# Two latent key/value blocks and two query blocks of a mixer as one Strassen quad ahead of the gate quads, with the convolution blocks regrouped

## The chip, the cores and the metric

The kernel runs on one core of one Trainium2 chip. The metric is the time of one execution in device microseconds. The engines are named as the profile names them: PE is TensorE, DVE is VectorE, ACT is ScalarE, POOL is GpSimd, SP issues the loads.

## The reference, cut to what matters

The trunk has two layers (DEPTH 2) over 512 tokens of width 1024. Each layer is a half-step SwiGLU, a mixer, a second half-step SwiGLU, and a per-layer embedding. The change is in the front of the mixer:

```
u = rmsnorm(h, mix_norm[i])
b_g, c_g, v_c, q_c, kv_c, k_r, g_conv, g_mla = jnp.split(u @ w_in[i], split_pts, axis=-1)
y_conv = short_conv_branch(b_g, c_g, v_c, conv_w[i], w_conv_out[i])
y_mla = mla_branch(q_c, kv_c, k_r, q_norm[i], kv_norm[i], ...)     # rmsnorm of q_c and kv_c first
merged = jax.nn.sigmoid(g_conv) * y_conv + jax.nn.sigmoid(g_mla) * y_mla
```

In blocks of 128 columns, w_in holds four blocks each for B, C and V of the convolution, three for the query latent q_c, two for the key/value latent kv_c, half a block for the rotary key k_r, and eight for each of the two gates. The output is the final RMSNorm of h, 512 x 1024.

## The kernel before, in words

Activations lie transposed: a block is 128 channels by 512 tokens. Each fp32 number is split into a rounded part (hi) and a rest (lo), so a plain projection of one block (`proj`, L275, and `mm3`, L266 to L270) is eight channel groups times three matmuls of 512 columns: hi with hi, hi with lo, lo with hi.

Weights come in tiles of 128 x 1024 (eight 128 x 128 blocks). SP loads them into ten raw buffers `st`; `Stream.split` (L58 to L73) makes `wh` with a cast on ACT (L71) and `wl` with a subtraction on DVE (L72). There are four buffers of `wh` and four of `wl`, so a split waits until PE has finished with the tile four before it.

A **quad** is a block of four output columns computed by a seven-product Strassen scheme over halves of the channels and halves of the tokens. `Quad.part` (L138 to L158) makes its seven weight tiles from four raw ones: seven splits, and four additions or subtractions of 128 x 1024 on DVE (L149, L152, L154, L157). `Sevens.step(n, j)` (L552) does product j of quad n in the order 1, 2, 6, 5, 7, 3, 4. Products 1, 2, 6, 3 and 4 are `joint` (L516): eight matmuls of 512 columns (L525) and eight of 256 (L529). Products 5 and 7 are `product` (L532): 24 matmuls of 256 columns (L538). Two of the sums are started by a **seed**: ACT copies 128 x 1024 from one PSUM buffer `b` into the buffer `a` or `d` (L543), both of which are the single buffer of the pool `ap`. Product 2 adds into `a` and so waits for its seed; product 5 adds into `d` and waits for its own. A seed also waits until DVE has read out what that buffer held before (L548). After product 2, 3 and 4, ACT copies one half (L547), DVE adds the other (L548) and scales by the row norm r; gates then go through a sigmoid on ACT. The token sums and differences that the quads read as moving operand come from `Halved.row` (L457 to L496): four subtractions or additions of 128 x 256 and three splits per row on DVE, and five operations on ACT, for four rows.

The mixer (`mixer`, L736) starts with the two kv blocks (L768), the rotary key (L771 to L776) and the mean square of h (`rms`, L340), whose result r scales all that follows. Then the three query blocks, the norms of the two latents (`lat_norm`, L760: a mean square through two matmuls, an inverse root on ACT, then scaling on DVE), and convolution blocks 0 to 3, each C, V, B. Product 1 of quad 0 stands after C of block 3, products 2 and 6 after its V. Four quads of gates follow, `step(n+1, 1)`, `step(n, 4)`, `step(n+1, 2)` and so on, with the projections of the convolution's output (`conv_out`, L806) between them.

PSUM has eight banks here: `bp` (two buffers of two banks, the `b` of the quads; also lent to convolution blocks), `ap` (one of two banks) and `mp` (two of one bank, `PS`). A tile of `PS` waits for the reader of the tile whose bank it takes. Instructions of one engine run in the order in which Tile's scheduler has put them; each engine's queue is strictly in that order.

Of the kernel before, what the change touches and what calls it, by code (L numbers as in the profile page):

```python
# [13 lines left out]
ALU = mybir.AluOpType  # L14
AX = mybir.AxisListType

P = 128
# [3 lines left out]
ROPE = 64  # L21
# [3 lines left out]
SCALE = float((NOPE + ROPE) ** -0.5)  # L25
# [157 lines left out]
def trunk_kernel(ctx, tc, dims, x, p, positions, gains, rope_c, final_row, weights, out):  # L183

    nc = tc.nc
# [14 lines left out]
    def G(name, dt=F32):  # L200
        return gp.tile([P, S], dt, tag="g", name=name)
# [28 lines left out]
    def PS(name):  # L230
        return banks.single.tile([P, 512], F32, tag="mm", name=name)
# [4 lines left out]
    def PB(name):  # L236
        return two(banks.chain, name)
# [4 lines left out]
    def halves(t):  # L242
        return [t[:, 0, :], t[:, 1, :]]
# [28 lines left out]
    def proj(tiles, vs, name, ps=None):  # L272
        ps = PS(name) if ps is None else ps
        o = ps[:, :vs[0][0].shape[1]]
        for k, (t, v) in enumerate(zip(tiles, vs)):  # L275
            mm3(o, W.get(t), v, k == 0, k == len(tiles) - 1)
        return ps

    def projs(cols_, vs, pss, part_by_part=False):

        for k, (vh, vl) in enumerate(vs):
            ws = [W.get(tiles[k]) for tiles in cols_]
            if k == 0 and part_by_part:
                for ps, (wh, _) in zip(pss, ws):
                    nc.tensor.matmul(ps, wh, vh, start=True, stop=False)
                for ps, (_, wl) in zip(pss, ws):
                    nc.tensor.matmul(ps, wl, vh, start=False, stop=False)
                for ps, (wh, _) in zip(pss, ws):
                    nc.tensor.matmul(ps, wh, vl, start=False, stop=False)
                continue  # L290
            for ps, w in zip(pss, ws):
                mm3(ps, w, (vh, vl), k == 0, k == len(vs) - 1)
        return pss
# [22 lines left out]
    def gain(nm, l, k):  # L316
        c = col_at[nm, l] + k
        return cols[:, c:c + 1]
# [23 lines left out]
    def rms(acc, n, name, scale=1.0, ps=None):  # L342

        ah, al = acc
        ps = PS(name + "ps") if ps is None else ps
        nc.tensor.matmul(ps, ones, ah, start=True, stop=False)
        nc.tensor.matmul(ps, ones, al, start=False, stop=True)
        r, t, ms = (rp.tile([P, S], F32, tag=g, name=name + w) for g, w in (("r", "r"), ("w", "t"), ("w", "ms")))

        nc.scalar.activation(r, ps, AF.Abs_reciprocal_sqrt, scale=1.0 / n, bias=eps_t)  # L350
        nc.scalar.activation(t, r, AF.Square)
        nc.scalar.activation(ms, ps, AF.Identity, scale=1.0 / n, bias=eps_t)
        nc.vector.scalar_tensor_tensor(t, t, -0.5 * scale, ms, ALU.mult, ALU.mult)
        nc.vector.scalar_tensor_tensor(r, t, 1.5 * scale, r, ALU.add, ALU.mult)
        return r
# [369 lines left out]
    def rope(src, cos, sin, name):  # L725

        t1, t2 = G(name + "t1"), G(name + "t2")
        for a in range(0, P, 64):
            for o, i in ((a, a + 32), (a + 32, a)):
                nc.scalar.copy(t2[o:o + 32, :], src[i:i + 32, :])  # L730
        nc.vector.tensor_tensor(t1, src, cos, ALU.mult)
        nc.vector.tensor_tensor(t2, t2, sin, ALU.mult)
        nc.vector.tensor_tensor(t1, t1, t2, ALU.add)
        return t1

    def mixer(l):  # L736
# [7 lines left out]
        o_gc = o_kr + ROPE  # L744
        o_gm = o_gc + D

        def lat_in(c0, width, nm):
            pss = halves(PB(f"{name}{nm}p")) + [PS(f"{name}{nm}p2")]
            return [proj(W.col("w_in", l, c0 + k * P, D), xs, None, pss[k]) for k in range(width // P)]

        def lat_scale(pss, nm):
            ts, sq = [], Squares(name + nm)
            for k, ps in enumerate(pss):
                t = G(f"{name}{nm}t{k}")
                nc.vector.tensor_tensor(t, ps, r, ALU.mult)
                ts.append(t)
                sq.add(t)
            return ts, sq.parts()

        def lat_norm(ts, acc, nm, scale=1.0):  # L760
            rl = rms(acc, len(ts) * P, name + nm, scale)
            for k, t in enumerate(ts):
                nc.vector.scalar_tensor_tensor(t, t, gain(nm, l, k), rl, ALU.mult, ALU.mult)
            return ts

        pkv = halves(PB(name + "kvp"))
        projs([W.col("w_in", l, o_kv + k * P, D) for k in range(KL // P)], xs, pkv)

        pkr = PS(name + "krp")
        kr_cols = W.col("w_in", l, (o_kr, o_kr), D)  # L770
        for k, (vh, vl) in enumerate(xs):  # L771
# [3 lines left out]
            nc.tensor.matmul(pkr, wa[:, t], vh, start=k == 0, stop=False)  # L775
            nc.tensor.matmul(pkr, wb[:, t], vl, start=False, stop=k == KD - 1)  # L776
        r = rms(acc, D, name)
        kvt = lat_scale(pkv, "kv")
        krn, krs = G(name + "krn"), G(name + "krs")
        nc.scalar.copy(krs[:ROPE, :], pkr[ROPE:, :])  # L780
        nc.vector.tensor_tensor(krs[:ROPE, :], pkr[:ROPE, :], krs[:ROPE, :], ALU.add)
        for o in (0, ROPE):
            nc.vector.tensor_tensor(krn[o:o + ROPE, :], krs[:ROPE, :], r[:ROPE, :], ALU.mult)
        qt = lat_scale(lat_in(o_q, QL, "q"), "q")
        kvt = lat_norm(*kvt, "kv")
        krt = rope(krn, cosT, sinT, name + "kr")
        ys = Halved("mix", l, name)


        yc = []  # L790
        r2 = G(name + "r2")
        nc.vector.tensor_tensor(r2, r, r, ALU.mult)

        gates = [None] * (2 * KD)

        def gate(n, f, c, src, t):
            at = slice(c * (S // 2), (c + 1) * (S // 2))
            nc.vector.tensor_tensor(t, src, r[:, at].unsqueeze(1).to_broadcast([P, 2, S // 2]), ALU.mult)
            for w in range(2):
                i = 4 * n + 2 * f + w  # L800
                if gates[i] is None:
                    gates[i] = G(f"{name}g{i}")
                nc.scalar.activation(gates[i][:, at], t[:, w, :], AF.Sigmoid)

        def conv_out(m):
            ps = proj(W.col("w_conv_out", l, m * P, CONV), yc, f"{name}cop{m}")  # L806
            nc.vector.tensor_tensor(gates[m], ps, gates[m], ALU.mult)


        step = Sevens("w_in", l, name + "g", ys.ys,  # L810
                      lambda n: [[o_gc + (4 * n + 2 * a_ + w) * P for w in range(2)] for a_ in range(2)], gate).step

        for k in range(CONV // P):
            last = k == CONV // P - 1
            pc = PS(f"{name}Cp{k}") if last else halves(PB(f"{name}Cp{k}"))[0]
            ps = proj(W.col("w_in", l, o_c + k * P, D), xs, None, pc)
            c = G(f"{name}c{k}")
            nc.vector.tensor_tensor(c, ps, r2, ALU.mult)
            if last:
                ys.row(k, xs)  # L820
                step(0, 1)
            ps = proj(W.col("w_in", l, o_v + k * P, D), xs, f"{name}Vp{k}")
            z = G(f"{name}z{k}")
            nc.vector.tensor_tensor(z, ps, c, ALU.mult)
            y = G(f"{name}y{k}")
            cw = [gain("conv", l * 3 + j, k) for j in range(3)]
            nc.scalar.mul(y, z, cw[2])
            nc.vector.scalar_tensor_tensor(y[:, 1:], z[:, :-1], cw[1], y[:, 1:], ALU.mult, ALU.add)
            nc.vector.scalar_tensor_tensor(y[:, 2:], z[:, :-2], cw[0], y[:, 2:], ALU.mult, ALU.add)
            if last:  # L830
                step(0, 2)
                step(0, 6)
            ps = proj(W.col("w_in", l, o_b + k * P, D), xs, f"{name}Bp{k}")
            b = G(f"{name}b{k}")
            nc.vector.tensor_tensor(b, ps, r, ALU.mult)
            nc.vector.tensor_tensor(y, y, b, ALU.mult)
            yc.append(split(y, f"{name}yc{k}"))
            if not last:
                ys.row(k, xs)
            if k == 1:  # L840
                qt = lat_norm(*qt, "q", SCALE)
        for j in (5, 7, 3):
            step(0, j)

        class Pair:
            def __init__(self, pr):
# [54 lines left out]
                assert self.vw or not nxt  # L901

        pairs = [Pair(pr) for pr in range(N_HEADS // 2)]
        n_last = KD // 2 - 1
        outs = list(range(KD - 1))

        def conv_outs(n):
# [2 lines left out]
            del outs[:n]  # L910

        for n in range(n_last):
            for n_, j_, n_out in ((n + 1, 1, n > 0), (n, 4, 0), (n + 1, 2, 0), (n + 1, 6, 1), (n + 1, 5, 0), (n + 1, 7, 0),
                                  (n + 1, 3, 1)):
                step(n_, j_)
                conv_outs(n_out)
                if (n_, j_) == (n_last, 2):
                    qc = [split(t, f"{name}qn{k}", paired=True) for k, t in enumerate(qt)]
                    kvc = [split(t, f"{name}kvn{k}") for k, t in enumerate(kvt)]
                    krh, krl = split(krt, name + "kr", paired=True)  # L920
# [356 lines left out]
```

## Time and profile before

| | |
|---|---|
| median of 3 runs | 2260.66 us (2260.35 to 2261.06) |
| the profiled execution, its own time | 2260.81 us |
| its span, first to last instruction | 2258.7 us |
| PE busy | 2246.9 us, 99% of the span |
| DVE busy | 1719.7 us, 76% |
| ACT busy | 1432.2 us, 63% |
| weight load of PE (PEld) | 1947.6 us, 86% |
| granted TensorE clock | 0.999 |
| the mixer of layer 0, first matmul of kv to start of product 1 of quad 0 | 351.88 to 438.58 us |
| the mixer of layer 0, from there to the last product of quad 3 | 438.58 to 549.50 us |

The ends of matmuls are modelled, so PE is read by the distance from one start to the next. The idle time of an engine other than PE costs nothing by itself. The lines that matter are shown in the prediction.

### The profile page before, as it was taken

To read this page: it belongs to the slowest core of one execution; us is meant where nothing else is said; L and a number is where in the kernel's file an instruction comes from. 1 tells how busy PE (TensorE), PEld (TensorE's weight loads), DVE (VectorE), ACT (ScalarE), POOL (GpSimd) and SP (SyncE) were. 2 spreads that over 40 slices of the span, in tenths; PEclk is the share of its full clock that TensorE was granted. 3 is DMA by queue.
4 is the path that set the end of the run, shared out by engine and by line. 5 is a ranking of instruction groups with operands and counts; after the bars stand their busy time and mean duration, and the time that the engine had idled before them with its cause. 6 is when DMAs were issued, how large, how long until landed. Compare 5 with 4: busy or idle time off the path is not lost.

```text
span 2258.7 us, 30986 instructions
## 1 busy us (share of the span) xinstructions
PE 2246.9 (99%) x12080; PEld 1947.6 (86%) x12080; DVE 1719.7 (76%) x2423; ACT 1432.2 (63%) x2220; POOL 37.3 (2%) x42
## 2 busy tenths in 40 slices
PE   9999999999999999999999999999999999999998
PEld 7888888888888888888888888888888888888887
DVE  8887767877876877776798777678879678777756
ACT  7666666566744666666676666655567457666664
POOL 0000000000200000000000000000001000000000
PEclk9999999999999999999999999999999999999999
DMA  5233332223122223333222333332322223333321
GB/s 215 96 105 103 112 122 95 73 95 102 48 103 84 88 99 103 104 112 131 84 94 95 102 105 110 112 103 75 103 75 75 94 75 103 102 105 105 111 94 38
DMA packets 63363, 223.05 MB, mean 99 GB/s; under 512 B 7280, under 2 KB 7280, under 8 KB 63216
## 3 DMA queue, kind: packets, MB, share of 16 engines
q1 hardware_dynamic: 62640, 220.28, 29.2%
q8 instruction: 95, 1.56, 0.3%
q10 hardware_dynamic: 576, 0.79, 0.1%
q14 instruction: 52, 0.43, 0.1%
HBM read 218.94 MB, written 2.10 MB: 98 GB/s over the span
## 4 chain that ended last, share of the span: by engine, by line
PE 99%; ACT 0%; DVE 0%; issue 0%; DVEq 0%; ACTq 0%
PE b1pd L268 2%; PE b0pd L268 2%; PE a1pd L268 2%; PE a0pd L268 2%; PE a1pd L269 2%; PE b0pd L269 2%; PE b1pd L269 2%; PE b1pd L270 2%; PE a1pd L270 2%; PE b0pd L270 2%; PE a0pd L269 2%; PE a0pd L270 2%; PE m0mop L268 1%; PE m0mop L269 1%; PE m1mop L268 1%; PE m1mop L270 1%
## 5 line engine op out<-in xcount | busy, mean ns | idle before, releaser
L72 DVE TENSOR_TENSOR wl<-st,wh 128x1024 fp32r<-128x1024 f32 (+1 forms) x504 | 610.2, 1213 | 322.4 <-ACT wh L71 321.4
L71 ACT CAST wh<-st 128x1024 fp32r<-128x1024 f32 (+1 forms) x503 | 523.8, 1044 | 420.5 <-issue 13.8
L152 DVE TENSOR_TENSOR st<-st,st 128x1024 f32<-128x1024 f32 x47 | 57.5, 1224 | 1.3
L72 DVE TENSOR_TENSOR wl<-s,wh 128x1024 fp32r<-128x1024 f32 x47 | 57.2, 1217 | 0.4 <-ACT wh L71 0.4
L154 DVE TENSOR_TENSOR s<-st,st 128x1024 f32<-128x1024 f32 x47 | 57.3, 1219 | 0.2
L149 DVE TENSOR_TENSOR st<-st,s 128x1024 f32<-128x1024 f32 x47 | 57.2, 1216 | 0.0
L157 DVE TENSOR_TENSOR st<-st,st 128x1024 f32<-128x1024 f32 x47 | 57.1, 1216 | 0.0
L71 ACT CAST wh<-s 128x1024 fp32r<-128x1024 f32 x47 | 48.9, 1041 | 8.2 <-PE a1p L269 2.6
L632 ACT ACTIVATE h<-a0pd 128x512 f32<-128x512 f32 x40 | 23.7, 596 | 17.7 <-PE a0pd L270 17.6
L632 ACT ACTIVATE h<-b1pd 128x512 f32<-128x512 f32 x40 | 23.8, 597 | 16.9 <-PE b1pd L270 16.7
L632 ACT ACTIVATE h<-a1pd 128x512 f32<-128x512 f32 x40 | 23.7, 596 | 16.5 <-PE a1pd L270 16.3
L632 ACT ACTIVATE h<-b0pd 128x512 f32<-128x512 f32 x40 | 23.7, 596 | 16.4 <-PE b0pd L270 16.3
L628 ACT ACTIVATE a0pd<-h 128x512 f32<-128x512 f32 x40 | 24.0, 601 | 2.5 <-DVE a010o L548 1.7
L628 ACT ACTIVATE b1pd<-h 128x512 f32<-128x512 f32 x40 | 24.0, 602 | 2.2 <-DVE b110o L548 1.4
L628 ACT ACTIVATE a1pd<-h 128x512 f32<-128x512 f32 x40 | 24.0, 601 | 2.2 <-DVE a110o L548 1.4
L628 ACT ACTIVATE b0pd<-h 128x512 f32<-128x512 f32 x40 | 24.0, 601 | 2.2 <-DVE b010o L548 1.4
L107 POOL MEMSET wh<- 128x256 f32 x4 | 1.1, 312 | 1180.6 <-DVE wl L72 1180.6
L270 PE MATMUL a0p<-a0x,wl 128*128 128x512 f32 x44 | 17.1, 389 | 0.0
L268 PE MATMUL a0p<-a0x,wh 128*128 128x512 f32 x44 | 17.1, 389 | 0.0
L269 PE MATMUL a0p<-a0x,wh 128*128 128x512 f32 x44 | 17.1, 389 | 0.0
L263 ACT ACTIVATE b0x<-h,cols 128x512 fp32r<-128x512 f32 x8 | 5.8, 724 | 13.3 <-DVE h L1027 13.3
L263 ACT ACTIVATE b1x<-h,cols 128x512 fp32r<-128x512 f32 x8 | 5.8, 724 | 13.3 <-DVE h L1027 13.3
(6807 smaller groups left out, 7498.1 us busy)
## 6 DMA issues: line engine op xcount, KB each, us to landing
st<-in_weights SPq DMA_DIRECT2D x406, 512.0 KB, 3.3
h<-in_x SPq DMA_DIRECT2D x8, 256.0 KB, 5.5
st<-in_weights SPq DMA_DIRECT2D x7, 256.0 KB, 5.4
out<-e1d SPq DMA_DIRECT2D x4, 256.0 KB, 2.1
out<-fh SPq DMA_DIRECT2D x3, 256.0 KB, 2.3
e0pi<-in_p SPq DMA_DIRECT2D x2, 256.0 KB, 4.5
e1pi<-in_p SPq DMA_DIRECT2D x2, 256.0 KB, 4.4
fg<-in_final_row SPq DMA_DIRECT2D x2, 256.0 KB, 5.3
```

Source lines behind the costliest of these rows:

```text
L71: self.nc.scalar.copy(hi[:, w], src[:, w])
L72: self.nc.vector.tensor_tensor(lo[:, w], src[:, w], hi[:, w].bitcast(F32), ALU.subtract)
L149: tt(self.a12, self.a12, self.s, ALU.subtract)
L152: tt(self.a11, self.a11, self.a21, ALU.subtract)
L154: tt(self.s, self.a22, self.a11, ALU.subtract)
L157: tt(self.a21, self.a21, self.a22, ALU.add)
L263: nc.scalar.activation(hi, src, AF.Copy, scale=scale)
L268: nc.tensor.matmul(ps, wh, vh, start=first, stop=False, skip_group_check=seeded)
L269: nc.tensor.matmul(ps, wh, vl, start=False, stop=False, skip_group_check=seeded)
L270: nc.tensor.matmul(ps, wl, vh, start=False, stop=last, skip_group_check=seeded)
L628: nc.scalar.mul(ps, h[m], 2.0)
L632: nc.scalar.mul(h[m], ps, 0.5)
```

## The change: what it does

It takes the two kv blocks and the first two query blocks out of the plain projections and makes them quad 0; the four quads of gates become quads 1 to 4 (`n_last` goes from 3 to 4). The third query block stays a plain projection (`pq2`) and now opens the mixer, ahead of the rotary key. The rows of `Halved` are made during convolution blocks 0 and 1. Blocks 0 and 1 stand ahead of quad 0; C, V and B of block 2 stand after products 1, 2 and 6 of quad 0, those of block 3 after products 1, 2 and 6 of quad 1. C of blocks 2 and 3 takes a `PS` bank; before, only block 3's did. The mean squares and norms of the two latents move behind products 6, 5, 7 and 3 of quad 1. Everything is done in both layers.

```diff
-        pkv = halves(PB(name + "kvp"))
-        projs([W.col("w_in", l, o_kv + k * P, D) for k in range(KL // P)], xs, pkv)
+        pq2 = proj(W.col("w_in", l, o_q + 2 * P, D), xs, None, halves(PB(name + "qp"))[0])
...
-        qt = lat_scale(lat_in(o_q, QL, "q"), "q")
-        kvt = lat_norm(*kvt, "kv")
...
+            if n == 0:
+                for w in range(2):
+                    nc.vector.tensor_tensor(lats[2 * f + w][:, at], src[:, w, :], r[:, at], ALU.mult)
+                return
...
+            cs = [o_kv, o_kv + P, o_q, o_q + P] if n == 0 else [c0 + i * P for i in range(4)]
...
+            pc = halves(PB(f"{name}Cp{k}"))[0] if k < 2 else PS(f"{name}Cp{k}")
...
+        for j in (1, 2, 6, 5, 7, 3):
             step(0, j)
+            if j in (1, 2, 6):
+                next(convs[2])
...
-        n_last = KD // 2 - 1
+        n_last = KD // 2
...
-                conv_outs(n_out)
+                if n == 0:
+                    if j_ in (1, 2, 6):
+                        next(convs[3])
+                    if j_ == 6:
+                        kva = latents(kvt, "kv")
+                    if j_ == 5:
+                        qa = latents(qt, "q")
+                    if j_ == 7:
+                        lat_norm(kvt, kva, "kv")
+                    if j_ == 3:
+                        lat_norm(qt, qa, "q", SCALE)
+                else:
+                    conv_outs(n_out)
```

**ACT, up to the seed of the second gate quad.** Before, this is the stretch in which quad 0 (gates) ends and quad 1 begins: `m0g0` is quad 0, `m0g1a` the seed that product 2 of quad 1 waits for, `wh` a weight cast, L803 the sigmoids.

```order
L71 CAST wh_4292<-st_4014 128x1024
L566 COPY m0g0c_4198<-m0g0d 128x512
L71 CAST wh_4318<-st_4267 128x1024
L71 CAST wh_4349<-s 128x1024
L803 ACTIVATE m0g_4230<-m0g0c_4198 128x256
L803 ACTIVATE m0g_4232<-m0g0c_4198 128x256
L547 COPY m0g0o_4255<-m0g0d 128x512
L71 CAST wh_4374<-st_4372 128x1024
L543 COPY m0g1a<-m0g1b 128x1024
```

In the changed kernel the same stretch lies between quad 1 (now the first gates) and quad 2; `m0kv` and `m0q` belong to the norms of the latents, L776 are the sigmoids, and the seed is `m0g2a`.

```order
L350 ACT_TABLE_LOAD
L350 ACTIVATE m0kvr<-m0kvps,eps_t 128x512
L260 CAST m0qah<-m0qacc 128x512
L351 ACTIVATE m0kvt<-m0kvr 128x512
L776 ACT_TABLE_LOAD
L776 ACTIVATE m0g_4271<-m0g1c_4227 128x256
L776 ACTIVATE m0g_4273<-m0g1c_4227 128x256
L352 ACTIVATE m0kvms<-m0kvps,eps_t 128x512
L547 COPY m0g1o_4309<-m0g1d 128x512
L71 CAST wh_4417<-s 128x1024
L547 COPY m0g1o_4380<-m0g1b 128x512
L543 COPY m0g2a<-m0g2b 128x1024
```

Two loads of an activation table and the norm of the kv latent now stand in ACT's queue ahead of the seed, where there were casts, one pair of sigmoids and one copy; a second such pair of loads, for the query latent, stands between this seed and the next one (`m0g2d`).

**DVE, up to the reader of V of convolution block 1.** Before, between the reader of its C (L818) and of its V (L824) stands one weight split.

```order
L470 TENSOR_TENSOR m0t_3668<-m0x_3667 128x256
L484 TENSOR_TENSOR m0t_3668<-m0y_3673,m0x_3667 128x256
L485 TENSOR_TENSOR m0u_3674<-m0t_3668,m0x_3667 128x256
L486 TENSOR_TENSOR m0u_3674<-m0y_3673,m0u_3674 128x256
L261 TENSOR_TENSOR m0t0l<-m0t_3668,m0t0h 128x512
L261 TENSOR_TENSOR m0u_6_3681<-m0u_3674,m0u_6_3681 128x256
L261 TENSOR_TENSOR m0u_4_3684<-m0u_3674,m0u_4_3684 128x256
L818 TENSOR_TENSOR m0c_3718<-m0Cp_3687,m0r_3557 128x512
L72 TENSOR_TENSOR wl_3866<-st_3863,wh_3865 128x1024
L824 TENSOR_TENSOR m0z_3751<-m0Vp_3720,m0c_3718 128x512
```

In the changed kernel the rows just ahead of the two readers (now L807 and L811) are those of the third row of `Halved` (`m0t`, `m0u`) and a part of quad 0's weights (L149).

```order
L149 TENSOR_TENSOR st_3701<-st_3701,s 128x1024
L484 TENSOR_TENSOR m0t_3539<-m0y_3544,m0x_3538 128x256
L485 TENSOR_TENSOR m0u_3545<-m0t_3539,m0x_3538 128x256
L486 TENSOR_TENSOR m0u_3545<-m0y_3544,m0u_3545 128x256
L261 TENSOR_TENSOR m0t2l<-m0t_3539,m0t2h 128x512
L261 TENSOR_TENSOR m0u_6_3552<-m0u_3545,m0u_6_3552 128x256
L261 TENSOR_TENSOR m0u_4_3555<-m0u_3545,m0u_4_3555 128x256
L807 TENSOR_TENSOR m0c_3589<-m0Cp_3558,m0r_3376 128x512
L72 TENSOR_TENSOR wl_3788<-st_3785,wh_3787 128x1024
L811 TENSOR_TENSOR m0z_3622<-m0Vp_3591,m0c_3589 128x512
```

Three rows of `Halved` (0, 1 and 2) and quad 0's four weight sums now stand ahead of the reader of V of block 1; before, it was one row and none of the sums. C of block 2 takes the `PS` bank that this reader frees.

More of the change, by code (lines that the diff above doesn't have):

```diff
@@ L745, in mixer @@
         o_gm = o_gc + D
[L747 to L764, printed above, removed]
-        pkv = halves(PB(name + "kvp"))
-        projs([W.col("w_in", l, o_kv + k * P, D) for k in range(KL // P)], xs, pkv)
+        pq2 = proj(W.col("w_in", l, o_q + 2 * P, D), xs, None, halves(PB(name + "qp"))[0])
         pkr = PS(name + "krp")
@@ L777, in mixer, with take @@
         r = rms(acc, D, name)
[L778 to L783, printed above, removed]
-        qt = lat_scale(lat_in(o_q, QL, "q"), "q")
-        kvt = lat_norm(*kvt, "kv")
-        krt = rope(krn, cosT, sinT, name + "kr")
-        ys = Halved("mix", l, name)
-        yc = []
         r2 = G(name + "r2")
         nc.vector.tensor_tensor(r2, r, r, ALU.mult)
+        ys = Halved("mix", l, name)
+        lats = [G(f"{name}lat{i}") for i in range(5)]
+        kvt, qt = lats[:2], lats[2:]
         gates = [None] * (2 * KD)
-        def gate(n, f, c, src, t):
+        def take(n, f, c, src, t):
             at = slice(c * (S // 2), (c + 1) * (S // 2))
+            if n == 0:
+                for w in range(2):
+                    nc.vector.tensor_tensor(lats[2 * f + w][:, at], src[:, w, :], r[:, at], ALU.mult)
+                return
             nc.vector.tensor_tensor(t, src, r[:, at].unsqueeze(1).to_broadcast([P, 2, S // 2]), ALU.mult)
             for w in range(2):
-                i = 4 * n + 2 * f + w
+                i = 4 * (n - 1) + 2 * f + w
                 if gates[i] is None:
@@ L803, in gate, with columns, latents, lat_norm @@
                 nc.scalar.activation(gates[i][:, at], t[:, w, :], AF.Sigmoid)
+        def columns(n):
+            c0 = o_gc + 4 * (n - 1) * P
+            cs = [o_kv, o_kv + P, o_q, o_q + P] if n == 0 else [c0 + i * P for i in range(4)]
+            return [cs[:2], cs[2:]]
+        step = Sevens("w_in", l, name + "g", ys.ys, columns, take).step
+        def latents(ts, nm):
+            sq = Squares(name + nm)
+            for t in ts:
+                sq.add(t)
+            return sq.parts()
+        def lat_norm(ts, acc, nm, scale=1.0):
+            rl = rms(acc, len(ts) * P, name + nm, scale)
+            for k, t in enumerate(ts):
+                nc.vector.scalar_tensor_tensor(t, t, gain(nm, l, k), rl, ALU.mult, ALU.mult)
+        yc = []
         def conv_out(m):
@@ L807, in conv_out, with conv @@
             nc.vector.tensor_tensor(gates[m], ps, gates[m], ALU.mult)
[L810 to L815, printed above, removed]
+        def conv(k):
+            pc = halves(PB(f"{name}Cp{k}"))[0] if k < 2 else PS(f"{name}Cp{k}")
             ps = proj(W.col("w_in", l, o_c + k * P, D), xs, None, pc)
@@ L818, in mixer @@
             nc.vector.tensor_tensor(c, ps, r2, ALU.mult)
-            if last:
-                ys.row(k, xs)
-                step(0, 1)
+            yield
             ps = proj(W.col("w_in", l, o_v + k * P, D), xs, f"{name}Vp{k}")
@@ L829, in mixer @@
             nc.vector.scalar_tensor_tensor(y[:, 2:], z[:, :-2], cw[0], y[:, 2:], ALU.mult, ALU.add)
-            if last:
-                step(0, 2)
-                step(0, 6)
+            yield
             ps = proj(W.col("w_in", l, o_b + k * P, D), xs, f"{name}Bp{k}")
@@ L837, in mixer @@
             yc.append(split(y, f"{name}yc{k}"))
[L838 to L842, printed above, removed]
+            yield
+        convs = [conv(k) for k in range(CONV // P)]
+        next(convs[0])
+        nc.vector.tensor_tensor(qt[2], pq2, r, ALU.mult)
+        krn, krs = G(name + "krn"), G(name + "krs")
+        nc.scalar.copy(krs[:ROPE, :], pkr[ROPE:, :])
+        nc.vector.tensor_tensor(krs[:ROPE, :], pkr[:ROPE, :], krs[:ROPE, :], ALU.add)
+        for o in (0, ROPE):
+            nc.vector.tensor_tensor(krn[o:o + ROPE, :], krs[:ROPE, :], r[:ROPE, :], ALU.mult)
+        ys.row(0, xs)
+        for k in range(2):
+            for _ in convs[k]:
+                if k == 0:
+                    ys.row(1, xs)
+                    break
+            for _ in convs[k]:
+                pass
+            ys.row(2 + k, xs)
+        krt = rope(krn, cosT, sinT, name + "kr")
+        for j in (1, 2, 6, 5, 7, 3):
             step(0, j)
+            if j in (1, 2, 6):
+                next(convs[2])
         class Pair:
@@ L912, in mixer @@
         for n in range(n_last):
-            for n_, j_, n_out in ((n + 1, 1, n > 0), (n, 4, 0), (n + 1, 2, 0), (n + 1, 6, 1), (n + 1, 5, 0), (n + 1, 7, 0),
+            for n_, j_, n_out in ((n + 1, 1, n > 1), (n, 4, 0), (n + 1, 2, 0), (n + 1, 6, 1), (n + 1, 5, 0), (n + 1, 7, 0),
                                   (n + 1, 3, 1)):
                 step(n_, j_)
-                conv_outs(n_out)
+                if n == 0:
[11 more added lines that the diff above has]
+                    conv_outs(n_out)
                 if (n_, j_) == (n_last, 2):
```

## The prediction

> **What bounds the kernel now.** I read the page first: busy shares, then the chain that ended last.
>
> ```profile
> span 2258.7 us, 30986 instructions
> PE 2246.9 (99%) x12080; PEld 1947.6 (86%) x12080; DVE 1719.7 (76%) x2423; ACT 1432.2 (63%) x2220; POOL 37.3 (2%) x42
> ...
> PE 99%; ACT 0%; DVE 0%; issue 0%; DVEq 0%; ACTq 0%
> ```
>
> PE is busy for 2246.9 of 2258.7 us and carries 99% of the chain. A change gains what it takes from PE's queue, and loses every wait that it puts there. Next I asked which waits PE has at all (waiting line, releaser, us in total, times, longest).
>
> ```profile
> PE a02a L525 <- ACT a02a L543: 1.7, 1, 1.7
> PE a02d L538 <- ACT a02d L543: 1.2, 1, 1.2
> ```
>
> Apart from one at the very start, these two are all, and neither lies in a mixer: there PE never waits. Both are of one kind, a product that waits for its seed (L543 on ACT), in the first SwiGLU. So the kernel can wait there, and the question is whether ACT and DVE still keep ahead of PE in the changed mixer. Their load by stages (columns: window, its length, busy us of PE, PEld, DVE, ACT and POOL with counts, clock, DMA share, GB/s):
>
> ```profile
> 383.70:438.60 54.90, 54.90 (x244) 45.41 (x243) 45.87 (x67) 27.14 (x41) 0.00 (x0) 1.00 0.20 68
> 457.80:477.60 19.80, 19.80 (x130) 18.09 (x130) 19.45 (x22) 13.72 (x20) 0.00 (x0) 1.00 0.25 84
> ```
>
> The first is convolution blocks 0 to 2 and C of block 3: DVE has 9 us to spare in 55. The second is the seam between two quads: DVE is full (19.45 of 19.80 us), and ACT has 6 us left.
>
> **What PE gains.** Starts on PE, from its timeline (start, length, line, tile):
>
> ```profile
> 366.39 0.39 PE L346 MATMUL m0ps<-m0ah,ones 128*128 128x512 f32 x1
> ...
> 366.86 0.40 PE L268 MATMUL m0qp<-m0x,wh 128*128 128x512 f32 x1
> ...
> 400.01 0.39 PE L268 MATMUL m0Cp<-m0x,wh 128*128 128x512 f32 x1
> ...
> 405.45 0.39 PE L268 MATMUL m0Vp<-m0x,wh 128*128 128x512 f32 x1
> ...
> 471.98 2.00 PE L525 MATMUL m0g1a<-m0x,wh 128*128 128x512 f32 x8
> ...
> 474.77 2.00 PE L525 MATMUL m0g1b<-m0u,wh 128*128 128x512 f32 x8
> ...
> 480.31 0.28 PE L538 MATMUL m0g1d<-m0t0h,wh 128*128 128x256 f32 x1
> ...
> 483.18 0.28 PE L538 MATMUL m0g1b<-m0t0h,wh 128*128 128x256 f32 x1
> ...
> 486.06 2.00 PE L525 MATMUL m0g1d<-m0x,wh 128*128 128x512 f32 x8
> ```
>
> A plain block takes 405.45 - 400.01 = 5.44 us, so the four that go took 21.76. A joint product takes 474.77 - 471.98 = 2.79, the other two 2.87 and 2.88, so the quad that comes takes 5 x 2.79 + 2.87 + 2.88 = 19.70. Saved: 2.06 us per layer, 4.1 us in both. This is certain: the matmuls of the kernel are counted, and those of the mixer run back to back. It is also the most that there is to win, and 4.1 us is 0.18%, inside the 0.2% (4.5 us) that a measurement of this kernel can tell from no change.
>
> **What it adds, and where it is hidden.** Per layer ACT gets three more casts of 1024, two seeds and four table loads, DVE three more splits and four weight sums. Away from the places below, that lies beside PE's matmuls: quads 2 to 4 stand as quads 1 to 3 stood, and quads 0 and 1 have three convolution projections each (16.3 us of PE) between their products. The loads are as many as before, and no row quoted here waits for DMA. The opening is tighter, since one query block (0.68 us per channel group at 5.44 / 8) eats the normed tiles faster than two kv blocks did:
>
> ```profile
> 351.88 0.39 PE L268 MATMUL m0kvp<-m0x,wh 128*128 128x512 f32 x1
> ...
> 354.85 0.75 DVE L264 SCALAR_TENSOR_TENSOR m0x<-h,cols,m0x 128x512 fp32r<-128x512 f32 x1
> ...
> 356.88 0.69 DVE L261 TENSOR_TENSOR m0al<-m0acc,m0ah 128x512 fp32r<-128x512 f32 x1 [0.69 <-ACT m0ah L260]
> ```
>
> The last tile is done at 355.6 and is now wanted at 351.88 + 7 x 0.68 = 356.6; the mean square's operand is done at 357.6 and wanted after the query block and the key (16 matmuls, 3.6 us), at 361. Nothing; without that 1 us of cover it would cost what the tile is late.
>
> **Term one: C of block 2.** Its `PS` bank is freed by the reader of V of block 1 on DVE, which stands behind three rows of `Halved` and the sums of quad 0. Durations on DVE, by starts:
>
> ```profile
> 371.77 0.69 DVE L354 SCALAR_TENSOR_TENSOR m0r<-m0t,m0r 128x512 f32<-128x512 f32 x1
> 372.50 1.29 DVE L755 TENSOR_TENSOR m0kvt<-m0kvp,m0r 128x512 f32<-128x512 f32 x2
> ...
> 403.28 0.42 DVE L470 TENSOR_TENSOR m0t<-m0x 128x256 f32<-128x256 f32 x1
> ...
> 406.15 0.68 DVE L818 TENSOR_TENSOR m0c<-m0Cp,m0r 128x512 f32<-128x512 f32 x1
> ...
> 460.52 0.68 DVE L261 TENSOR_TENSOR m0yc3l<-m0y,m0yc3h 128x512 fp32r<-128x512 f32 x1
> 461.12 1.22 DVE L152 TENSOR_TENSOR st<-st,st 128x1024 f32<-128x1024 f32 x1
> 462.25 1.22 DVE L72 TENSOR_TENSOR wl<-st,wh 128x1024 fp32r<-128x1024 f32 x1
> ```
>
> So 0.60 us for 512, 1.13 for 1024, 2.87 for a row (406.15 - 403.28), 0.73 where one needs the one before. Call the first matmul of the mean square (366.39 before) X. PE goes on at X + 0.47, has six convolution projections (32.6) and product 1 (2.8), and wants the bank at X + 35.9. DVE starts what follows r at X + 6.1 (372.50 - 366.39). Up to the end of that reader stand 14 of 512 (8.4), ten of 1024 (11.3: six splits, four sums), three rows (8.6), two waits for ACT of 0.7 and five direct dependences of 0.13 more: 30.3, so X + 36.4. PE waits **0.5 us** per layer. Bounds: 0, if the pitches are 2% shorter; 1.5, if ACT's casts come late by as much again as in the two waits counted. The rest of this stage has room: the last row is wanted only by product 6, 14 us later.
>
> **Term two: the seed of quad 2.** ACT's rows, for the queue shown in the order:
>
> ```profile
> 366.72 1.05 ACT L71 CAST wh<-st 128x1024 fp32r<-128x1024 f32 x1 [2.94 <-PE m0krp L776]
> 367.79 1.28 ACT L350 ACT_TABLE_LOAD   x1
> 369.09 0.69 ACT L350 ACTIVATE m0r<-m0ps,eps_t 128x512 f32<-128x512 f32 x1
> ...
> 373.25 0.63 ACT L333 ACTIVATE m0kvacc<-m0kvt 128x512 f32<-128x512 f32 x1
> 373.82 0.63 ACT L336 ACTIVATE m0kvsq<-m0kvt 128x512 f32<-128x512 f32 x1
> ...
> 385.88 0.68 ACT L352 ACTIVATE m0kvms<-m0kvps,eps_t 128x512 f32<-128x512 f32 x1
> 386.44 0.62 ACT L260 CAST m0qah<-m0qacc 128x512 fp32r<-128x512 f32 x1
> ...
> 460.80 1.05 ACT L71 CAST wh<-st 128x1024 fp32r<-128x1024 f32 x1 [0.68 <-PE m0g0d L538]
> 461.75 0.58 ACT L566 COPY m0g0c<-m0g0d 128x512 f32<-128x512 f32 x1
> 463.68 1.05 ACT L71 CAST wh<-st 128x1024 fp32r<-128x1024 f32 x1 [1.35 <-PE m0g0b L538]
> ...
> 466.98 0.73 ACT L803 ACTIVATE m0g<-m0g0c 128x256 f32<-128x256 f32 x2 [0.28 <-DVE m0g0c L798]
> 467.61 0.57 ACT L547 COPY m0g0o<-m0g0d 128x512 f32<-128x512 f32 x1
> ...
> 469.90 1.00 ACT L543 COPY m0g1a<-m0g1b 128x1024 f32<-128x1024 f32 x1 [0.38 <-DVE m0g0o L548]
> ```
>
> Before, the seed is done at 470.9 and its product begins at 471.98: 1.1 us of slack. Now count from the end of product 7 of quad 1. PE has two mean squares (2 x 0.47) and three joint products (8.4) before product 2 of quad 2, which it wants at 9.3. ACT begins a cast at 0.1, when product 7 frees its buffer (as at 463.68), and is never idle until the seed: cast 0.95, copy 0.5, three squares 1.7, table load 1.3, inverse root 0.6, cast 0.55, square 0.6, table load 1.3, sigmoids 0.65, identity 0.55, copy 0.5, cast 0.95, copy 0.5, seed 1.0, together 11.65. So the seed is done at 11.75, and PE waits **2.4 us** per layer. Of that, 2.6 are the two table loads; without them the seed would just be in time. Bounds: 0.5, if ACT gets two operations earlier than I count; 4, if it also waits for DVE in between, as in the 0.28 and 0.38 of the rows above.
>
> The row of the load says that ACT's cast ends at 367.77 and the load begins at 367.79, and the next operation follows 0.02 us after it: 1.30 us in all. [...]
>
> **Term three: the next seed, m0g2d.** Between the two seeds ACT has three pairs of sigmoids 1.9, two table loads 2.6, three short operations and a copy 2.2, two casts 2.0 and the seed 1.0: 9.7 us. PE has products 2 and 6 (5.6) and 18 matmuls of conv_out (4.1 at 5.44 / 24 each): 9.7. A tie: **0.2 us**, bounds 0 and 2.6.
>
> **The sum.** Per layer -2.06 + 0.5 + 2.4 + 0.2 = +1.0, in both layers +2.1. On the profiled execution (2260.8, which is 0.15 us over the median of 2260.66) that gives 2262.9, on the median 2262.8.
>
> **The rivals.** *PE waits nowhere.* Then the time is 2260.7 - 4.1 = 2256.6. For it speaks that no seed in the mixer is late now, and that each wait is a small difference of sums over 12 and 36 us. Against it speaks that ACT's queue to the seed would have to be 20% shorter than its rows. Chance 0.15.
>
> *ACT's second pair of loads is not covered* (slower). The last sigmoids ahead of m0g2d need DVE's scaling, which stands behind a step that needs ACT's identity; every such exchange lands on a tie. If the two loads (2.6 us) come through whole, it is 2 x 2.6 more: 2268.0. The time leaves the 0.2% once the waits of a layer exceed 2.06 + 2.26 = 4.3 us. For it speaks the full DVE of the seam. Chance 0.20.
>
> *A switch of table costs twice its row.* If ACT stood still as long again after each of the four loads, the first seed would be 2.6 later, the second too: 2262.8 + 2 x 5.2 = 2273.2. The rows speak against it, 0.02 us between load and next operation. Chance 0.03. [...]
>
> **How the numbers follow.** The forecast has the remaining 0.62. Range 2257.0 to 2268.0: from just above the case without waits to the slower rival, which leaves out about a tenth on either side. Its own range is 2259.5 to 2266. Faster by over 0.2% needs 4.5 us and PE offers 4.1: 0.04. Slower takes the second and third rival and a little of the forecast's tail: 0.25. Same: 0.71.
>
> **What would show it.** In the changed profile: a plain C row starting right after the latent quad's first joint product with an idle time of about 0.5 us, released by DVE's reader (L811); product 2 of quad 2 (m0g2a) waiting about 2.4 us for L543; eight more table loads; latent quad products of 2.79 and 2.87 us. Wrong would be: no PE wait at m0g2a (then ACT's queue was overcounted), waits elsewhere, as on a split L72 in quad 2 (then DVE binds), or a wait in only one layer.

## The result and the profile after

The changed kernel takes 2265.75 us (median; 2263.87 to 2267.95), the kernel before on the same chip 2260.78 us (2260.32 to 2261.29): a ratio of 1.0021, 95% interval 1.0014 to 1.0029. That is 5.0 us more. The profiled execution took 2264.55 us.

The page of the changed kernel, busy time and the shares of the chain by engine:

```profile
span 2262.4 us, 31150 instructions
...
PE 2244.4 (99%) x12144; PEld 1947.5 (86%) x12144; DVE 1739.5 (77%) x2453; ACT 1454.1 (64%) x2246; POOL 37.4 (2%) x42
...
PE 94%; DVE 3%; ACT 2%; issue 0%; DMA 0%; SPq 0%; ACTq 0%; DVEq 0%
```

By these rows, in which the ends of matmuls are modelled, PE has 2.5 us less to do than before (2246.9), and yet the span is 3.7 us longer. DVE and ACT now hold 5% of the chain. That is not 5% of waiting, since the chain follows their queues back a long way from each place where PE stands still; but PE does stand still in places. Which places, the waits of PE tell, here those of 0.9 us and more (waiting line, releaser, us in total, times, longest):

```profile
PE m0g2a L525 <- ACT m0g2a L543: 2.1, 1, 2.1
PE m1g2a L525 <- ACT m1g2a L543: 2.1, 1, 2.1
PE a02a L525 <- ACT a02a L543: 1.7, 1, 1.7
PE a02d L538 <- ACT a02d L543: 1.2, 1, 1.2
PE idle L376 <- DVE hpi L305: 1.0, 1, 1.0
PE m1Cp L268 <- DVE m1z L811: 0.9, 1, 0.9
PE m0Cp L268 <- DVE m0z L811: 0.9, 1, 0.9
```

Four of these are new, two in each layer: C of block 2 for DVE's reader of V, and product 2 of quad 2 for its seed on ACT. Nothing waits at the second seed, `m0g2d`. The first of the two places on PE and on DVE (timeline: start, length, engine, line, operation; in brackets idle time and what ended it):

```profile
395.97 1.11 PE L529 MATMUL m0g0b<-m0x,wl 128*128 128x256 f32 x8
398.00 0.47 PE L268 MATMUL m0Cp<-m0x,wh 128*128 128x512 f32 x1 [0.92 <-DVE m0z L811]
```

```profile
367.14 0.69 DVE L758 TENSOR_TENSOR m0r<-m0r 128x512 f32<-128x512 f32 x1
...
377.75 0.75 DVE L815 SCALAR_TENSOR_TENSOR m0y<-m0z,cols,m0y 128x511 f32<-128x511 f32 x1 [0.79 <-ACT m0y L814]
...
389.34 0.69 DVE L261 TENSOR_TENSOR m0yc0l<-m0y,m0yc0h 128x512 fp32r<-128x512 f32 x1 [0.69 <-ACT m0yc0h L260]
390.30 1.23 DVE L72 TENSOR_TENSOR wl<-st,wh 128x1024 fp32r<-128x1024 f32 x1 [0.26 <-ACT wh L71]
...
397.17 0.68 DVE L811 TENSOR_TENSOR m0z<-m0Vp,m0c 128x512 f32<-128x512 f32 x1
```

DVE has only three idle moments between the first of these rows and the reader, all for ACT, and reaches it at 397.85. PE is done with product 1 of quad 0 at 396.93 (8 x 0.12 behind 395.97) and starts C at 398.00. The second place, on ACT and on PE:

```profile
461.96 1.05 ACT L71 CAST wh<-st 128x1024 fp32r<-128x1024 f32 x1
...
465.08 1.28 ACT L350 ACT_TABLE_LOAD   x1
466.38 0.69 ACT L350 ACTIVATE m0kvr<-m0kvps,eps_t 128x512 f32<-128x512 f32 x1
...
468.11 1.28 ACT L776 ACT_TABLE_LOAD   x1
469.41 0.72 ACT L776 ACTIVATE m0g<-m0g1c 128x256 f32<-128x256 f32 x2
...
472.50 1.03 ACT L543 COPY m0g2a<-m0g2b 128x1024 f32<-128x1024 f32 x1
...
481.26 1.00 ACT L543 COPY m0g2d<-m0g2b 128x1024 f32<-128x1024 f32 x1
```

```profile
470.39 1.11 PE L529 MATMUL m0g1b<-m0u,wl 128*128 128x256 f32 x8
473.58 2.11 PE L525 MATMUL m0g2a<-m0x,wh 128*128 128x512 f32 x8 [2.08 <-ACT m0g2a L543]
...
483.38 0.30 PE L538 MATMUL m0g2d<-m0t0h,wh 128*128 128x256 f32 x1
```

ACT is never idle from 461.96 to the end of the seed at 473.53, and two of its rows are table loads. PE had its last product issued at 471.35. The second seed is done at 482.26, and PE comes to it at 483.38: 1.1 us to spare. Between the two seeds ACT has one weight cast, at 474.06.

These waits account for most of what the profiled execution takes longer, but not for the median. The runs of the changed kernel stand in groups by the mean granted TensorE clock that each shows: 2263.87 to 2265.02 us at 0.999 (six runs), 2265.72 to 2266.41 at 0.998 (five), 2267.46 to 2267.95 at 0.997 (three). The kernel before shows 0.999; the little that lacks there is the end of the kernel, where PE has no more work and the clock falls (in its profile it is 0.50 from 2255.7 us on, in that of the changed kernel from 2257.6). The steps between the groups are about 1.8 us, and the median of all runs stands in the middle one. The median of the six runs at 0.999 is 2264.3 us; that is the changed kernel at full clock. So there are three questions: whether the two waits have the causes that the prediction gave them, what each is worth, and what lowers the clock.

### The profile page after: what moved, and what is told of

The parts are those of the page before. It is cut to its first block, busy times and chain, and to the rows that moved or that the text cites. A ratio compares the mean times of both kernels' runs of the same rounds, so it can differ in the third digit from the quotient of the medians.

```text
span 2262.4 us, 31150 instructions
## 1 busy us (share of the span) xinstructions
PE 2244.4 (99%) x12144; PEld 1947.5 (86%) x12144; DVE 1739.5 (77%) x2453; ACT 1454.1 (64%) x2246; POOL 37.4 (2%) x42
## 4 chain that ended last, share of the span: by engine, by line
PE 94%; DVE 3%; ACT 2%; issue 0%; DMA 0%; SPq 0%; ACTq 0%; DVEq 0%
PE b1pd L268 2%; PE b0pd L268 2%; PE a1pd L268 2%; PE a0pd L268 2%; PE a1pd L269 2%; PE b0pd L269 2%; PE b1pd L269 2%; PE b0pd L270 2%; PE b1pd L270 2%; PE a1pd L270 2%; PE a0pd L269 2%; PE a0pd L270 2%; PE m0mop L268 1%; PE m1mop L268 1%; PE m1mop L269 1%; PE m0mop L270 1%
## 5 line engine op out<-in xcount | busy, mean ns | idle before, releaser
L152 DVE TENSOR_TENSOR st<-st,st 128x1024 f32<-128x1024 f32 x49 | 59.9, 1223 | 1.3
L149 DVE TENSOR_TENSOR st<-st,s 128x1024 f32<-128x1024 f32 x49 | 59.7, 1218 | 0.0
L157 DVE TENSOR_TENSOR st<-st,st 128x1024 f32<-128x1024 f32 x49 | 59.6, 1217 | 0.0
```

What stands on the lines that cost most here:

```text
L149: tt(self.a12, self.a12, self.s, ALU.subtract)
L152: tt(self.a11, self.a11, self.a21, ALU.subtract)
L157: tt(self.a21, self.a21, self.a22, ALU.add)
```

## The experiments

Theory: the wait of C of block 2 is the bank behind DVE's reader, the wait of quad 2 is the two table loads in ACT's queue, the two add up with PE's saving, and the clock is lowered by PE's own pause of some 2 us. Rivals: PE would wait elsewhere once one wait is gone (DVE binds); the saving is not there; the clock drops belong to the table loads or to the new order and not to the pause.

**c2_bank: C of block 2 gets a bank of the pool `bp`, as C of blocks 0 and 1 do.**

```diff
-            pc = halves(PB(f"{name}Cp{k}"))[0] if k < 2 else PS(f"{name}Cp{k}")
+            pc = halves(PB(f"{name}Cp{k}"))[0] if k < 3 else PS(f"{name}Cp{k}")
```

> One letter of the change is undone: C of block 2 gets a bank of the two-bank pool (as before the change) instead of a PS bank. Theory (two waits per layer, and a clock that falls in some runs after the long one): the wait of about 0.9 us of PE for DVE's reader L811 goes, the 2.1 us wait for the seed m0g2a stays. The lowest runs fall from about 2263.9 to about 2262.0, and the runs still spread over 3 to 4 us, in steps of about 1.8 us, with the granted clock at 0.999, 0.998 and 0.997. Rival (the spread belongs to the short wait, or to neither wait): the spread is gone, or the lowest run does not fall.

Measured: 2263.90 us (2263.49 to 2265.45), ratio to before 1.0015, interval 1.0006 to 1.0024. The waits at C are gone, those at `m0g2a` and `m1g2a` stay at 2.1 us, and none is new. But no run shows a clock of 0.999: six are at 0.998 (2263.49 to 2263.90) and five at 0.997 (2264.48 to 2265.45). So the lowest run did not fall to the 2262.0 that was expected. The profiled execution, one of those at 0.998, has the drop in sight. PE in stretches of 3.41 us, the length of that drop, two around the first layer's pause and three around the second's (stretch, its length, busy us with instructions, granted clock, DMA share, GB/s; the drop is the fourth):

```profile
467.74:471.15 3.41, 2.79 (x17) 1.00 0.00 0
471.15:474.56 3.41, 1.93 (x8) 1.00 0.02 5
1587.31:1590.72 3.41, 1.33 (x10) 1.00 0.00 0
1590.72:1594.13 3.41, 3.41 (x11) 0.50 0.05 7
1594.13:1597.55 3.42, 3.42 (x23) 1.00 0.41 146
```

PE stands still from 1588.2 to 1590.3. At 1590.72 the granted clock falls to half, and comes back 3.41 us later. The product that runs meanwhile shows it, against the same product of the first layer, where the pause was as long and the clock stayed (duration of one matmul: least, median, most):

```profile
L525 PE MATMUL m1g2a<-m1x,wh x8: 497/632/632, 1590.3 to 1593.1; 128*128 128x512 f32 x8
```

```profile
L525 PE MATMUL m0g2a<-m0x,wh x8: 389/391/499, 472.6 to 474.3; 128*128 128x512 f32 x8
```

A matmul of 632 ns instead of 391; by an estimate, half a clock for 3.41 us is worth 1.7 us, about the step between the groups. That the expected gain was there, and that the clock took it back, follows only with the gains measured below, under `both`.

**no_tables: the norms of the latents take a function that needs no table load.** The kernel leaves out the inverse root, so its latents are scaled by another factor.

```diff
-    def rms(acc, n, name, scale=1.0, ps=None):
+    def rms(acc, n, name, scale=1.0, ps=None, func=AF.Abs_reciprocal_sqrt):
...
-            rl = rms(acc, len(ts) * P, name + nm, scale)
+            rl = rms(acc, len(ts) * P, name + nm, scale, func=AF.Square)
```

> The inverse root of the two latent norms is replaced by Square, which needs no other table: the latents are scaled by a wrong factor, all instructions but the four table loads per layer remain. Theory: the two loads ahead of the seed (2.6 us) are the wait of 2.1 us, so PE no longer waits at m0g2a; the wait of 0.9 us at C of block 2 stays. Lowest run about 2259.6, spread under 1.2 us as in the kernel before, clock 0.999 in every run. Rival (ACT's other added work or DVE carries the wait): a wait of 1 us or more is left at m0g2a, lowest run 2261.5 or more. Rival on the spread (not due to the long pause): 3 to 4 us of spread remain.

Measured: 2259.53 us (2259.32 to 2260.17), ratio 0.9995, interval 0.9986 to 1.0003; every run at 0.999. The profile has 24 table loads, that of the changed kernel 32. No wait at quad 2, the two at C of block 2 as before.

**late_norm: the norms as they were, but called behind product 5 of quad 2, past its first seed.**

```diff
-                    if j_ == 7:
-                        lat_norm(kvt, kva, "kv")
-                    if j_ == 3:
-                        lat_norm(qt, qa, "q", SCALE)
                 else:
                     conv_outs(n_out)
+                    if (n, j_) == (1, 5):
+                        lat_norm(kvt, kva, "kv")
+                        lat_norm(qt, qa, "q", SCALE)
```

> The two latent norms are moved from behind products 7 and 3 of quad 1 to behind product 5 of quad 2; everything is computed. The order shows one pair of table loads now behind the seed m0g2a and ahead of m0g2d, the other behind m0g2d. Theory: no wait at m0g2a; the 0.9 us at C of block 2 stays; lowest run about 2259.6, spread under 1.2 us, clock 0.999. Rival (the loads are paid wherever they stand): a wait of about 2 us at m0g2d, m0g3a or m0g3d takes its place, lowest run 2262 to 2264.

Measured: 2259.47 us (2259.09 to 2259.92), ratio 0.9994, interval 0.9985 to 1.0002; every run at 0.999. PE's waits in the mixers:

```profile
PE m1Cp L268 <- DVE m1z L811: 0.9, 1, 0.9
PE m0Cp L268 <- DVE m0z L811: 0.9, 1, 0.9
```

And ACT around the first seed:

```profile
469.99 1.00 ACT L543 COPY m0g2a<-m0g2b 128x1024 f32<-128x1024 f32 x1 [0.81 <-DVE m0g1o L548]
470.90 0.59 ACT L547 COPY m0g1o<-m0g1b 128x512 f32<-128x512 f32 x1
471.51 1.28 ACT L350 ACT_TABLE_LOAD   x1
472.80 0.69 ACT L350 ACTIVATE m0kvr<-m0kvps,eps_t 128x512 f32<-128x512 f32 x1
473.50 1.28 ACT L776 ACT_TABLE_LOAD   x1
```

Here the loads are all still made, with the rest of the norms behind the seed instead of ahead of it, and the time is that of the kernel which does without them. So it is their place in ACT's queue that costs, and nothing else about them. Against the changed kernel at full clock (2264.3) both gain 4.8 us, 2.4 per layer. And the pause of 0.9 us, which both keep, did not lower the clock: all 22 runs stand at 0.999.

**both: late_norm and c2_bank together.**

> late_norm and c2_bank together, everything computed. Theory: PE waits nowhere in the mixer, and the whole 4.1 us of the Strassen quad come through: 2256.7 us, spread under 1.2 us, ratio to the kernel before 0.998. Rival (something else than the two waits eats the gain): 2259 or more, no better than the sum of the two single edits.

Measured: 2257.16 us (2256.89 to 2258.08), ratio to before 0.9985, interval 0.9976 to 0.9994; every run at 0.999. PE's waits are the three that stand unchanged among those of the changed kernel above (1.7 and 1.2 us in the first SwiGLU, 1.0 at the very start), and no others.

No wait takes the place of the two: DVE does not bind behind them. This is the one version whose interval against before lies wholly under 1, by 3.6 us. Taking the wait at C away is worth 2259.47 - 2257.16 = 2.3 us here, 1.15 per layer. Whether the two waits add up, c2_bank can tell, which has only the long one: 2257.16 + 4.8 = 2262.0, and with one drop of the clock at 1.7 us 2263.7. Its six runs at 0.998 have a median of 2263.65.

**pause_1, pause_3, pause_5, before_pause: the clock, by repeating the seed's copy.** From the kernel `both`, the copy of quad 2's first seed is made two, three and four times (N). In before_pause, made from the kernel before, the copy of quad 1's first seed is made four times (1 stands for the 2 in the condition).

```diff
-            nc.scalar.copy(d[what].rearrange("p w t -> p (w t)"), d["b"].rearrange("p w t -> p (w t)"))
+            for _ in range(N if (self.w, n, what) == ("w_in", 2, "a") else 1):
+                nc.scalar.copy(d[what].rearrange("p w t -> p (w t)"), d["b"].rearrange("p w t -> p (w t)"))
```

> This kernel is the one with both waits taken away (2257.16 us, clock 0.999 in all its runs), and the copy of block 2's first seed, m0g2a and m1g2a, is made twice; the second copy writes the same values, so nothing is left out. ScalarE has between the copies one eviction (0.57 us), so TensorE should pause about 0.57 + 0.95 less 0.2 of cover = 1.35 us in front of block 2's first quad product, once in each layer; the table loads stay hidden. Theory of the pause alone (time lost is the pause and nothing else): 2257.2 + 2 x 1.35 = 2259.9 us, every run within 1.2 us, clock 0.999. Theory of the granted clock (a pause of about 2 us or more lets the clock drop in some runs, each drop costs about 1.8 us more): a pause of 1.35 us lies between the 0.97 us that has caused no drop and the 2.1 us that has, so either 2259.9 at 0.999 or, if the limit is below it, 2261.7 to 2263.5 at 0.998 to 0.997.

> As the kernel with the copy made twice, with the copy made three times; two activations of the gate (0.36 us each) fall between the second and the third. TensorE should pause about 1.35 + 0.72 + 0.95 = 3.0 us per layer. The pause alone: 2257.2 + 6.0 = 2263.2 us, clock 0.999, little spread. The granted clock: drops in most runs or in all, of 1.8 us each, so 2265.0 (one) to 2266.8 us (two), at 0.998 to 0.997, and the profile shows a stretch of matmuls at about twice their spacing soon after one of the pauses. A third theory, that the drops come of ScalarE's table loads in front of the seed and not of TensorE's pause, gives 2263.2 at 0.999, since in this kernel the loads come after the seed.

> As before with the copy made four times; a cast of 1.0 us falls between the third and the fourth, so TensorE should pause about 3.0 + 1.0 + 0.95 = 5.0 us per layer. The pause alone: 2257.2 + 10.0 = 2267.2 us, clock 0.999. The granted clock: two drops in every run, 2270.8 us at 0.997, and less spread than with the pause of 3 us, since none escapes. The table loads: 2267.2 at 0.999.

> The kernel before, in which TensorE's only waits in the mixers are short, with the seed m0g1a and m1g1a of its quad 1 copied four times, the same values each time. By its rows three more copies of 0.95 us, an eviction and two activations come to 4.8 us on ScalarE, of which about 1.1 us is covered, so TensorE pauses 3 to 3.7 us per layer in a place that has nothing to do with the change. The pause alone: 2260.8 + 6.0 to 7.4 = 2266.8 to 2268.2 us at 0.999. The granted clock: up to two drops more, 2268.6 to 2271.8 us at 0.998 to 0.997. If this kernel shows drops, neither the new order nor the table loads are needed for them.

Measured: 2259.22, 2258.91 and 2262.24 us, and 2261.41 for the kernel before with the copies (ratio 1.0002, interval 0.9993 to 1.0011). The pauses did not come about: in the order of PE other products now stand in front of the seed (in pause_1 six more matmuls of conv_out). So three of the four sums were far too high, and the first came near (2259.9 expected) without its pause. The waits of `pause_1` and `pause_3` in the mixers are 0.8 and 0.7 us in all; what else makes them 2.1 and 1.8 us longer than `both` stays open. The longest waits in the mixers of the kernel with four copies, first layer (the second has 0.9 and 0.5):

```profile
PE m0qps L346 <- DVE m0g L801: 1.0, 1, 1.0
...
PE m0g2a L525 <- ACT m0g2a L544: 0.5, 1, 0.5
```

So these runs tell nothing of pauses of 3 or 5 us. They say that waits of up to 1.0 us left the clock at 0.999, in all runs but one of pause_5 (2264.32 us, 0.998). So did the pause of 1.7 us in the first SwiGLU (`a02a`), which all kernels here have, the kernel before too.

**pause_loads_2 and pause_loads_3: the clock, by table loads, which the order does not reckon with.** From `both`; F is two functions, or three.

```diff
             d[what] = PA(f"{self.name}{n}{what}")
+            if (self.w, n, what) == ("w_in", 2, "a"):
+                for func in F:
+                    nc.scalar.activation(d[what][:, 0, :1], d["b"][:, 0, :1], func)
```

> The kernels with repeated copies gave no pause of the length wanted, since the scheduler counts the copies and puts other products into the gap. A table load it does not count. So here, from the kernel with both waits taken away (2257.16 us), two activations of one column each, of other functions, are put ahead of the seeds m0g2a and m1g2a into the seed's own buffer, which the copy then overwrites, so that nothing is left out. ScalarE switches its table four times ahead of the copy; TensorE has 16 other products of 0.23 us to do before it needs the seed. By the rows of the kernel without waits the copy ends at about 476.4 us, TensorE comes to it at 473.0: a pause of 3.4 us in each layer. The pause alone: 2257.2 + 2 x 3.5 = 2264.2 us, every run at 0.999 and within 1.2 us. The granted clock: in most runs or in all one or two drops of about 1.8 us each, so 2266.0 to 2267.8 us at 0.998 to 0.997, and a stretch of matmuls at about double spacing within a few us behind the pause.

> As the kernel with two such activations, with three: six table loads ahead of the copy, a pause of about 6.5 us in each layer. The pause alone: 2257.2 + 2 x 6.6 = 2270.4 us at 0.999. The granted clock: a drop behind every pause, 2274.0 us at 0.997 or below in every run, with less spread than at 2 to 3 us.

Measured: 2271.22 us (2270.23 to 2271.39) at 0.996 to 0.997, and 2277.49 us (2276.38 to 2278.38) at 0.994 to 0.996, on another chip, where the kernel before takes 2260.75 us. PE does pause this time, in two pieces. The larger waits with two activations, in the first layer (the second has the same):

```profile
PE m0qps L346 <- DVE m0g L803: 2.1, 1, 2.1
...
PE m0g2a L525 <- ACT m0g2a L546: 1.6, 1, 1.6
```

The pauses alone are 2 x (2.1 + 1.6) = 7.4 us and would give 2264.6; the run takes 6.6 us more. With three activations the waits are 2.1 and 4.8 us in the first layer, 2.1 and 4.4 in the second; they alone would give 2270.6, and the run takes 6.9 us more. PE and its clock in stretches, in the first layer of that kernel and then of the one with three activations:

```profile
470.00:472.00 2.00, 2.00 (x11) 1.00 0.61 168
472.00:474.00 2.00, 0.34 (x2) 1.00 0.23 94
474.00:475.40 1.40, 0.73 (x2) 1.00 0.00 0
475.40:478.80 3.40, 2.00 (x5) 0.50 0.03 5
478.80:482.20 3.40, 3.40 (x14) 0.50 0.49 154
482.20:484.00 1.80, 1.80 (x9) 0.99 0.01 5
```

```profile
472.70:476.10 3.40, 0.72 (x2) 1.00 0.02 5
476.10:479.50 3.40, 0.00 (x0) 0.50 0.00 0
479.50:482.90 3.40, 2.88 (x7) 0.50 0.00 0
482.90:485.00 2.10, 2.10 (x15) 0.99 0.74 244
```

In both the clock is at half for 6.8 us here, twice the 3.4 us of the drop in c2_bank; in the second layer of the kernel with three activations it is so for 10.2 us (1599.10 to 1609.34). It fell here without the latent norms' loads ahead of the seed, and without an idle stretch as long as the drop: in the 3.4 us before it fell PE was still busy for about 1.1 and 0.72 us. The drops were expected to cost 1.8 us each, and cost more, since the clock here stayed down for 6.8 and 10.2 us. With two activations most of that is paid in the product behind the pause, whose 16 matmuls start over 5.3 us (476.8 to 482.1) instead of 2.8.

That both kernels with added loads show drops would also fit the theory that the loads themselves lower the clock. Against it stand late_norm and both, which make 32 loads, as the changed kernel does, against 24 before, without a pause of over 1 us in the mixers and without a drop. The first layer of c2_bank stands against it too: it has the same two loads ahead of the same pause as the second, and no drop. A long pause in a mixer without table loads ahead of it is in no run here.

## Why the prediction was right or wrong

The time lies within the range and 3 us over the number given. It stands at the edge of what was forecast as no change: a ratio of 1.0021 against a bound of 1.002, with an interval (1.0014 to 1.0029) that holds both sides. The direction, both places and their causes were right; what follows goes by the steps.

**PE's saving** (2.06 us per layer, "certain"): the quad's products stand at their length, and with all waits gone the kernel gains 3.6 of the 4.1 us. The missing 0.5 us is less than the interval of that ratio; where it goes stays open.

**The opening** at nothing: right; no wait of PE there in either layer.

**Term one, C of block 2** (0.5 us, bounds 0 to 1.5): right in place, releaser and cause, as c2_bank shows, and too small: 1.07 us in the rows (398.00 - 396.93), 1.15 by late_norm against both. PE came to the bank at the time that was counted (X = 361.03 in this profile, 361.03 + 35.9 = 396.93). DVE started at X + 6.1 as counted (367.14), and needed 30.7 us where 30.3 had been counted. Of the two waits of 0.7 for ACT that the count had, both came (0.79 and 0.69); a third, 0.26 in front of a weight split, was not in it. And PE takes 0.15 more to go on after the release.

**Term two, the seed m0g2a** (2.4 us, bounds 0.5 to 4): right. ACT's queue took 11.6 us from the cast at 461.96 to 473.53, against 11.65 counted. The row of the wait says 2.1, but PE's queue was through with the products in front at 471.35 and the first matmul behind started at 473.58, 2.2 us; no_tables and late_norm give back 2.4 per layer. Together they show that it is the loads.

**Term three, the seed m0g2d** (0.2, bounds 0 to 2.6): the seed is 1.1 us early, so nothing. Both did start together, as counted: ACT had done the first seed at 473.53 and PE went on at 473.58. PE took 9.8 us to this seed (483.38), where 9.7 had been counted, its 18 matmuls of conv_out in front. ACT took 8.7 (482.26) and not 9.7: of the two casts in the count only one stands between the seeds, and the next behind the second, from 482.20 on. So the tie was off by one cast (0.95 us), and that it fell to the good side is luck.

**The rivals.** That PE waits nowhere fell at once with the waits' rows; what it would have given, 2256.6, is nearly what `both` gives. The uncovered second pair of loads did not show: 1.1 us of cover is left. The table switch at twice its row fell: 465.08 + 1.28 = 466.36, and the next operation starts at 466.38.

**What the sum lacked.** Its terms give +1.0 per layer; in the runs at full clock it is (2264.3 - 2260.8) / 2 = 1.75. Of the difference 0.65 is term one and 0.25 what the saving fell short, less 0.2 for term three: 1.7 in all. The remaining 1.5 us between 2264.3 and the median is not in any term: it is the granted clock. The step that failed is that a wait was priced at its length. The pause of 2.1 us in the second layer of c2_bank's profile cost 2.1 us and a stretch of 3.41 us at half clock behind it. In the changed kernel, by an estimate from their mean clock and their times, eight of fourteen runs had at least one such stretch. That the median still lies in the forecast's own range, 2259.5 to 2266, is in part luck: the range held nothing for the clock, and the three runs at 0.997 lie above it.

## What to carry to other kernels

Price a wait that a change puts into TensorE's queue by more than its length: behind one of the two pauses of 2.1 us in c2_bank's profile the clock was at half for 3.41 us, worth an estimated 1.7 us more, while the pauses of up to 1.7 us in the kernels without longer ones left it at 0.999 here, in all runs but one. When the runs of one kernel fall into groups, set their times against the mean granted clock before you explain the median by the waits of one profiled execution. A step that switches ACT's table belongs behind the next copy that TensorE waits for: moving the two norms past one seed made the kernel 4.8 us shorter, and with a bank of the other pool for one projection too the regrouping is worth 0.15%.

## What the runs showed of the hardware that was not expected

The granted clock went to half for 3.41 us in c2_bank (1590.72 to 1594.13), for 6.8 us in the first layer of the two kernels with added loads (475.4 to 482.2 and 476.1 to 482.9), and for 10.24 us in the second layer of pause_loads_3 (1599.10 to 1609.34). In the 3.4 us before it fell, PE had been idle for some 2.1 us (c2_bank), 2.3 (3.4 less 1.07, pause_loads_2) and 2.7 us (3.4 less 0.72, pause_loads_3). In the first layer of pause_loads_2 PE was busy for 2.0 of the first 3.4 us at half clock and for all of the second, in that of pause_loads_3 for none of the first and for 2.88 of the second; then the clock came back.

The same pause of 2.1 us did not lower the clock in the first layer of c2_bank (470.5 to 472.6), nor in either layer of the changed kernel's profile, where the clock is 1.00 from 466 to 478 and from 1586 to 1598 us. At the end of the kernels too the idle time ahead of the fall differs: by its modelled end PE's last matmul is done at 2250.75 in the kernel before and at 2254.50 in the changed one, and the clock falls at 2255.7 and 2257.6, so 4.9 and 3.1 us later. What makes the clock fall behind one pause and not behind another as long, and why six runs of the changed kernel escaped and none of c2_bank, is not shown by these runs.
